# Sums over a head's 64 channels: from float32 matmuls with 64x64 blocks to two float32r passes with a 128x128 block matrix, the parts made by GpSimd

## The chip, the core and the metric

The kernel runs on one core of a Trainium2 chip. A core has a matrix engine (TensorE, PE in the profile), VectorE (DVE), ScalarE (ACT), GpSimd (POOL) and SyncE (SP, which only issues transfers here). They run side by side and wait for one another through semaphores; each takes its own instructions in a fixed order. The metric is the device time of one execution in microseconds (us), lower is better.

## The reference

Two layers of a bidirectional encoder on 256 tokens of width 2048. A layer normalises its input, multiplies it with one wide matrix, and feeds two groups of heads. Group A, sixteen heads of 64 channels, is the one that matters here (shortened):

```python
kk = heads(kf * k_k)
kk = kk * lax.rsqrt(jnp.maximum(jnp.sum(kk * kk, -1, keepdims=True), 1e-24))   # the key sum
...
for d, rev in enumerate((False, True)):
    decay = ...; a = jax.nn.sigmoid(...)
    kd = heads(kf * (1.0 + (a - 1.0) * k_a))
    y = y + wkv_scan(rh, heads(decay), kd, vh, kk, heads(a), rev)
    bonus = bonus + jnp.sum(rh * kd * rkf, -1, keepdims=True)                   # the bonus sum
yn = ...            # y normalised over the head's channels
out = yn + bonus * vh
```

Two sums run over the 64 channels of a head: one normalises the keys, one gives the bonus. Group B is a windowed attention. Both results are gated, joined, multiplied with an output matrix and added to the input.

## The kernel before

Channels lie on the 128 partitions and the 256 tokens along the columns. Two heads of 64 channels share the partitions, so group A is worked off in eight pairs, p = 0 to 7, in each of the two layers.

**The projections.** Every float32 product with the big matrices is made of three float32r matmuls (L290 to L292, tile `pm`): both operands are split into a float32r part `hi` and the rest `lo`, and hi·hi, hi·lo and lo·hi are summed. ScalarE makes the weight's `hi` (L220), VectorE its `lo` (L222). These matmuls form a long stream of steps, `S.run(n)`, three matmuls of 128x128 weights and 256 columns to a step.

**Windows and slots.** The rest of the work is cut into pieces and laid between the steps. A window holds 64 steps and is cut into 14 slots; at the head of a slot every generator that is due there runs one piece, then 4 or 5 steps follow. `scans(w)` lists the generators of window w with the slots in which they run. In the steady windows these are, for four different pairs at once:

- `scan_p`, pair w-1: prepares keys, decays and the bonus. It has two slot lists, here [6, 13] and [4, 5, 6, 7, 8, 9, 10, 11, 13]. In slot 4 it squares the keys (`sq`, tile `t`), in slot 6 the first list issues the key sum (`pk`) and the second then the decay factors PP and IP and the reciprocal, in slot 11 VectorE multiplies the bonus product (`km`, tile `lw`, two instructions), in slot 13 the first list issues the bonus sum (`pbn`) and the second `bv`, which reads it.
- `scan_i`, pair w-2 in all slots and pair w-3 in slots 0 and 1: inverts the 64x64 blocks of the delta rule (matmuls L866, L833 into `pq`, L875 into `pd`).
- `scan_b`, pair w-3 in slots 1 to 13 and pair w-4 in slots 1 to 4: the scan over the chunks (L923 to L953). In slot 12 it squares its output with sums (L964), VectorE adds the epsilon (`yv`, L965), GpSimd raises it to the power -0.5 (L966), and in slot 13 VectorE applies that (`ysq`).

The first pair of a layer has its own slots (`STAGE_P0`).

**What sets the order.** TensorE's order is that of the program, by hand. The other engines' order is made at build time by a planner: it follows the program with its own clock and gives an engine that comes free the ready instruction with the earliest place in the program. `high_priority(offset=n)` lets an instruction count as n places earlier: 95 for all of `scan_b` (`PRIO_B`), 40 for `lo`. The wrappers `PA` and `PV` (class `InTurn`) pin an instruction behind everything traced before it on its engine. The power at L966 goes to GpSimd directly, without such a pin. An engine stops at an instruction whose input isn't there, and everything behind it on that engine waits too.

**The head sums.** `head_sums` makes two matmuls, one for each head, 64 partitions into 64, with plain float32 operands and a 64x64 block of ones taken from the constant `bones`. Each shows as two matmul records in the profile (four for a head sum: 64 records of `pk` and 64 of `pbn` for 16 pairs).

**Tiles.** Tiles with one tag share its buffers in turn; a new one waits until the one before it in the buffer has been read. `ip` holds IP, `th` a pair's gate TH, both with one buffer. The results of head sums lie in PSUM, in a pool of two buffers that `scan_p` and `scan_i` share.

Of the kernel before, what the change touches and what calls it, by code (L numbers as in the profile page):

```python
# [9 lines left out]
F32 = mybir.dt.float32  # L10
F32R = mybir.dt.float32r
# [47 lines left out]


def _layout():
    names = ["ident", "ones", "bones", "cen", "gmf", "gmb"]
    off = {n: 128 * i for i, n in enumerate(names)}
    n = 128 * len(names)
    off["inv"] = n
    off["sgn"] = n + 1
    n += 2
    off["band"] = n
    n += 512
    off["lvl"] = n  # L70
    n += 64 * len(LEVELS)
    off["eye"] = n
    return off, n + 64
# [23 lines left out]
def make_consts():  # L97
    c = np.zeros((128, C_N), np.float32)
    r = np.arange(128)
    blk = (r[:, None] // 64 == r[None, :] // 64).astype(np.float32)  # L100
    put = lambda n, v: c.__setitem__((slice(None), slice(C_OFF[n], C_OFF[n] + v.shape[1])), v)
    put("ident", np.eye(128, dtype=np.float32))
    put("ones", np.ones((128, 128), np.float32))
    put("bones", blk)
    put("cen", np.eye(128, dtype=np.float32) - blk / 64.0)
    jj, tt = (r % 64)[:, None], np.arange(64)[None, :]
    put("gmf", np.concatenate([jj < tt, jj <= tt], 1).astype(np.float32))
    put("gmb", np.concatenate([jj > tt, jj >= tt], 1).astype(np.float32))
    band = np.zeros((128, 2, 256), np.float32)
    i, k = r[:, None], r[None, :]  # L110
    band[:, 0, 128:] = np.where(k <= i, 0.0, NEG)
    band[:, 1, :128] = np.where(k >= i, 0.0, NEG)
    put("band", band.reshape(128, 512))
    import jax.numpy as jnp

    inv = np.asarray(jnp.power(10000.0, -jnp.arange(32, dtype=jnp.float32) / 32))
    c[:, C_OFF["inv"]] = inv[r % 32]
    c[:, C_OFF["sgn"]] = np.where(r % 64 < 32, -1.0, 1.0)
    m = np.zeros((128, len(LEVELS), 2, 32), np.float32)
    row = r % 64  # L120
    cols = np.arange(64)
    for li, b in enumerate(LEVELS):
        lo = cols[(cols // b) % 2 == 0]
        up = cols[(cols // b) % 2 == 1]
        m[:, li, 0] = row[:, None] // b == lo[None, :] // b + 1
        m[:, li, 1] = row[:, None] // b == up[None, :] // b - 1
    put("lvl", m.reshape(128, -1))
    put("eye", (row[:, None] == cols[None, :]).astype(np.float32))
    return c
# [3 lines left out]
def hybrid_trunk_kernel(ctx, tc, xT, wi, wv, wo, par, fing, dup, iup, sink, pos, cst, out):  # L133
# [24 lines left out]
    def st(tag, shape, dt=F32, bufs=1):  # L158
        return sp.tile([128, *shape], dt, tag=tag, name=tag, bufs=bufs)
# [11 lines left out]
    PR = cp.tile([128, DEPTH, P_N], F32, name="PR")  # L171
    C = cp.tile([128, C_KEEP], F32, name="C")
    cc = lambda n, w=128: C[:, C_OFF[n] : C_OFF[n] + w]
    ident, ones, bones, cen = (cc(n) for n in ("ident", "ones", "bones", "cen"))
    gm = (cc("gmf"), cc("gmb"))

    def bigt(dt, name):
# [56 lines left out]
        def __getattr__(self, name):  # L234
            return lambda *a, **k: tc.keep_in_program_order(getattr(self.engine, name)(*a, **k))

    PA, PV = InTurn(A), InTurn(V)

    class Stream:

# [74 lines left out]
    MSK = cp.tile([128, NC, 64], F16, name="MSK")  # L315
    EYE, NEYE, EYE2 = (cp.tile([128, 64], F16, name=n) for n in ("EYE", "NEYE", "EYE2"))
    band = cp.tile([128, 512], BF16, name="band")
    FG = cp.tile([128, NKT], F32, name="FG")
    SK = cp.tile([128, DEPTH * 16], F32, name="SK")
    COS = cp.tile([128, T], F32, name="COS")  # L320
# [2 lines left out]
    def setup():  # L323
# [45 lines left out]
        V.memset(MSK, 1.0)  # L369
        V.memset(MSK[:, :, 0:1], 0.0)  # L370
        V.tensor_copy(band, cin[:, 0:512])
        V.tensor_copy(EYE, cin[:, 512 + 64 * NL : 576 + 64 * NL])
        V.tensor_scalar(NEYE, EYE, -1.0, None, op0=ALU.mult)
        V.tensor_scalar(EYE2, EYE, 2.0, None, op0=ALU.mult)
# [262 lines left out]
    def layer(l):  # L637
# [16 lines left out]
            PE.matmul(o, w[0], x[1], start=False, stop=False)  # L654
            PE.matmul(o, w[1], x[0], start=False, stop=True)

        def head_sums(o, x):
            for r in half:
                PE.matmul(o[r, 0:T], bones[r, r], x[r, 0:T], start=True, stop=True)

        def scan_p(p, t):
# [15 lines left out]
                PA.activation(TH[:, d * T : (d + 1) * T], pa[:, d * T : (d + 1) * T], AF.Tanh, scale=0.5, bias=dpm(NSH + 16, d * 8 + p))  # L679
            sq = st("t1", [T], bufs=3)  # L680
            PA.activation(sq, K, AF.Square, scale=prm(P_KK, p))
            KR = st("kkr", [T])
            PA.activation(KR, K, AF.Identity, scale=prm(P_KK, p))
            yield
# [46 lines left out]

            PV.tensor_tensor(km[:, 0:T], km[:, 0:T], km[:, T : 2 * T], op=ALU.add)
            PV.scalar_tensor_tensor(km[:, 0:T], km[:, 0:T], prm(P_RK, p), R, op0=ALU.mult, op1=ALU.mult)
            yield
            pb = wbank("pbn")
            head_sums(pb, km)
            yield
            t["bv"] = bv = st("bv", [T], bufs=3)
            PV.tensor_tensor(bv, pb[:, 0:T], VV, op=ALU.mult)
# [247 lines left out]
        def scans(w):  # L987

            gens = []
            prep = [(lag, at) for lag, at in enumerate(STAGE_P0) if lag == w] + [(1, at) for at in STAGE_P if w > 1]  # L990
            stages = [(4, scan_b, STAGE_B[1]), (3, scan_i, STAGE_I[1]), (3, scan_b, STAGE_B[0])]
            stages += [(lag, scan_p, at[0]) for lag, at in prep]
            stages += [(2, scan_i, STAGE_I[0])]
            stages += [(lag, scan_p, at[1]) for lag, at in prep]
            for lag, scan, at in stages:
                p = w - lag
                if 0 <= p < NP:
                    if (scan, p) not in chains:
                        chains[scan, p] = scan(p, L.ts[p])
                    gens.append((chains[scan, p], at))  # L1000
            return gens
# [210 lines left out]
```

## Time and profile before

| | |
|---|---|
| time, median of 3 runs | 1201.67 us (1200.83 to 1202.37) |
| the profiled execution: time, span | 1202.57 us, 1200.7 us |
| TensorE busy | 1171.1 us (98%) |
| VectorE, ScalarE, GpSimd busy | 903.2 us (75%), 766.5 us (64%), 19.2 us (2%) |
| matmuls of `pk` and `pbn` (L659) | 64 + 64 records, mean 402 ns |
| mean granted TensorE clock | 0.991 |

The span is from the first to the last instruction. The durations of matmuls overlap, since one begins while the one before it drains; the time that a matmul costs the stream is the distance between starts. "Idle before" is the time in which an engine had nothing to do ahead of an instruction, and behind the arrow stands what ended it. L235 is the line of the wrapper `InTurn`, so instructions with that line are told apart by their tiles.

### The profile page before, as it was taken

The page shows a single profiled execution, that of the slowest core. Times are in us where ns is not written, and L with a number is a line of the kernel's source. Part 1 is how long each engine was busy: PE and PEld are TensorE (multiplying, and loading weights), DVE is VectorE, ACT ScalarE, POOL GpSimd, SP SyncE. Part 2 cuts the span into 40 slices and gives each one's busy share as a digit, 9 for nine tenths or more (in the row PEclk, how much of TensorE's full clock was granted, in tenths as well). Part 3 has the DMA queues.
Part 4 walks back from the last instruction along what each step waited for, and adds up shares of the span by engine and source line. Part 5 has one row for each costly group of instructions (what it writes and reads, how often), then busy time and mean ns, then how long its engine had stood idle before and what let it go on. Part 6 is the DMA issues. An engine that isn't in the chain of part 4 may idle for free. (4 is left out here: it accounts for less than half of the span.)

```text
span 1200.7 us, 38176 instructions
## 1 busy us (share of the span) xinstructions
PE 1171.1 (98%) x16215; PEld 1088.0 (91%) x16215; DVE 903.2 (75%) x1987; ACT 766.5 (64%) x1920; POOL 19.2 (2%) x23
## 2 busy tenths in 40 slices
PE   8999999999999999999999999999999999999996
PEld 6988999999998889999999889999999988899996
DVE  6979778887877568866668878877887766786554
ACT  6756776776676557655555766776677665665553
POOL 0000000000000000000000000000000000000000
PEclk9999999999999999999999999999999999999998
DMA  7453233233323333477655343233323334345653
GB/s 270 148 169 123 97 101 127 92 112 114 108 93 118 120 114 131 143 236 235 211 187 172 124 131 113 91 114 114 111 96 105 117 120 133 113 148 184 211 186 122
DMA packets 60122, 166.71 MB, mean 139 GB/s; under 512 B 7696, under 2 KB 22704, under 8 KB 59952
## 3 DMA queue, kind: packets, MB, share of 16 engines
q1 hardware_dynamic: 59952, 164.27, 41.3%
q8 instruction: 127, 2.08, 0.7%
q14 instruction: 43, 0.35, 0.1%
HBM read 157.43 MB, written 4.19 MB: 135 GB/s over the span
## 5 line engine op out<-in xcount | busy, mean ns | idle before, releaser
L290 PE MATMUL pm<-XH,hi 128*128 128x256 f32 x1664 | 495.3, 298 | 2.4 <-ACT XH L182 2.1
L292 PE MATMUL pm<-XH,lo 128*128 128x256 f32 x1664 | 468.8, 282 | 4.8 <-DVE lo L222 4.8
L291 PE MATMUL pm<-XL,hi 128*128 128x256 f32 x1664 | 468.7, 282 | 0.3
L220 ACT ACTIVATE hi<-raw 128x512 fp32r<-128x512 f32 x560 | 327.9, 625 | 211.1 <-PE pm L291 137.5
L222 DVE TENSOR_TENSOR lo<-raw,hi 128x512 fp32r<-128x512 f32 x560 | 369.9, 687 | 100.8 <-ACT hi L220 93.9
L290 PEld LDWEIGHTS pm<-XH,hi 128*128 128x128 f32 x1664 | 314.6, 189 | 18.3 <-ACT XH L182 2.7
L292 PEld LDWEIGHTS pm<-XH,lo 128*128 128x128 f32 x1664 | 314.7, 189 | 6.5 <-DVE lo L222 6.4
L291 PEld LDWEIGHTS pm<-XL,hi 128*128 128x128 f32 x1664 | 315.1, 189 | 1.0 <-DVE XL L183 1.0
L290 PE MATMUL pm<-MH,hi 128*128 128x256 f32 x512 | 144.0, 281 | 0.0
L292 PE MATMUL pm<-MH,lo 128*128 128x256 f32 x512 | 143.8, 281 | 0.0
L291 PE MATMUL pm<-ML,hi 128*128 128x256 f32 x512 | 143.8, 281 | 0.0
L290 PEld LDWEIGHTS pm<-MH,hi 128*128 128x128 f32 x512 | 96.6, 189 | 0.8 <-issue 0.8
L292 PEld LDWEIGHTS pm<-MH,lo 128*128 128x128 f32 x512 | 96.6, 189 | 0.0
L291 PEld LDWEIGHTS pm<-ML,hi 128*128 128x128 f32 x512 | 96.6, 189 | 0.0
L869 ACT ACTIVATE QF<-pq 128x256 f16<-128x256 f32 x80 | 30.8, 385 | 25.0 <-PE pq L833 24.5
L876 DVE CAST_PREDICATED tv<-LV,pd 128x256 f16<-128x256 uint8 x80 | 34.3, 429 | 10.8 <-PE pd L875 10.0
L759 DVE TENSOR_TENSOR ge<-pg,C 128x1024 f32<-128x1024 f32 x32 | 39.1, 1221 | 3.9 <-PE pg L753 3.8
L941 ACT ACTIVATE suv<-pcc 64x128 f32<-64x128 f32 x128 | 34.2, 267 | 10.4 <-PE pcc L939 6.9
L1031 ACT ACTIVATE mv<-mv,mx 128x257 f32<-128x257 f32 x64 | 31.8, 501 | 11.5 <-DVE mx L1028 11.4
L925 ACT ACTIVATE rh<-pcc 128x128 f32<-128x128 f32 x64 | 17.5, 273 | 32.6 <-PE pcc L923 32.2
L753 PE MATMUL pg<-mv,bk 64*128 64x128 f32 x512 | 37.2, 285 | 0.0
L875 PE MATMUL pd<-QF,tt 64*64 64x32 f16 x1280 | 35.4, 186 | 0.9 <-ACT tt L837 0.8
(244 smaller groups left out, 1857.9 us busy)
## 6 DMA issues: line engine op xcount, KB each, us to landing
raw<-wi SPq DMA_DIRECT2D x208, 512.0 KB, 3.3
raw<-wo SPq DMA_DIRECT2D x64, 512.0 KB, 4.4
raw<-wv SPq DMA_DIRECT2D x8, 512.0 KB, 3.4
rrot<-u SPq DMA_DIRECT2D x80, 32.0 KB, 1.9
X<-xT SPq DMA_DIRECT2D x4, 512.0 KB, 7.1
vg<-xT SPq DMA_DIRECT2D x16, 128.0 KB, 3.6
xd<-vg SPq DMA_DIRECT2D x16, 128.0 KB, 3.5
vg<-xd SPq DMA_DIRECT2D x16, 128.0 KB, 3.3
```

Of the source, the lines that this page charges most:

```text
L220: A.activation(hi[:, q], raw[:, q], AF.Copy)
L222: V.tensor_tensor(lo[:, q], raw[:, q], hi[:, q].bitcast(F32), op=ALU.subtract)
L290: PE.matmul(pm, wh, rh[:, kk, :], start=(kk == 0), stop=False)
L291: PE.matmul(pm, wh, rl[:, kk, :], start=False, stop=False)
L292: PE.matmul(pm, wl, rh[:, kk, :], start=False, stop=(kk == 15))
L753: PE.matmul(pg[:, h, c * 128 : (c + 1) * 128], BK[half[h], d, c, 1 - h : 3 - h, :].rearrange("p s j -> p (s j)"), MV[half[h], d, c].rearra ...
L759: V.tensor_tensor(GEd(d), pg.rearrange("p h (c x) -> p h c x", c=NC), gm[d].unsqueeze(1).unsqueeze(1).to_broadcast([128, 2, NC, 128]), op= ...
L869: A.activation(t_sub(QF), flat4(pq[:, :, 0:128]), AF.Copy)
L875: PE.matmul(narrow(pd[:, d], h, c), hx(TT, d, c, h), sub(QF, h ^ d, d, c, d * b), start=True, stop=True)
L876: V.copy_predicated(t_sub(TC), t_mask, flat4(pd[:, :, 0:128]))
L941: A.activation(here(h), pc[half[h], 1], AF.Copy)
L1031: A.activation(Sc[:, h, q, 0:257], Sc[:, h, q, 0:257], AF.Exp, scale=0.125, bias=mx[:, q : q + 1], accum_out=den[:, q : q + 1])
```

## The change

The block matrix of ones leaves the constants and becomes a float32r tile `BONES` of 128x128, zero outside the two 64x64 blocks, built once by ScalarE. A head sum is now two matmuls over all 128 partitions, accumulated in the same place: the block matrix with the float32r part of the input, then with the rest. A new function `parts` makes these two on GpSimd, a copy that rounds to float32r and a subtract that reads the copy, through a new wrapper `PG` that pins them behind what was traced before on GpSimd. The parts of the squared keys are made in slot 4 in tag `ip`, those of the bonus product in slot 11 in tag `th`. In `scans`, the first slot list of `scan_p`, which holds the two head sums, moves in front of `scan_b` and the older `scan_i`.

```diff
-    names = ["ident", "ones", "bones", "cen", "gmf", "gmb"]
+    names = ["ident", "ones", "cen", "gmf", "gmb"]
...
-    PA, PV = InTurn(A), InTurn(V)
+    PA, PV, PG = InTurn(A), InTurn(V), InTurn(G)
...
+    BONES = cp.tile([128, 128], F32R, name="BONES")
...
+        A.activation(BONES, ones, AF.Copy, scale=0.0)
+        for r in half:
+            A.activation(BONES[r, r], ones[r, r], AF.Copy)
...
-        def head_sums(o, x):
-            for r in half:
-                PE.matmul(o[r, 0:T], bones[r, r], x[r, 0:T], start=True, stop=True)
+        def parts(x, tag):
+
+            hl = st(tag, [2, T], F32R)
+            PG.tensor_copy(hl[:, 0], x)
+            PG.tensor_tensor(hl[:, 1], x, hl[:, 0].bitcast(F32), op=ALU.subtract)
+            return hl
+
+        def head_sums(o, hl):
+            for i in range(2):
+                PE.matmul(o[:, 0:T], BONES, hl[:, i], start=(i == 0), stop=(i == 1))
...
             PA.activation(sq, K, AF.Square, scale=prm(P_KK, p))
+            sq = parts(sq, "ip")
...
             PV.scalar_tensor_tensor(km[:, 0:T], km[:, 0:T], prm(P_RK, p), R, op0=ALU.mult, op1=ALU.mult)
+            bonus = parts(km[:, 0:T], "th")
             yield
             pb = wbank("pbn")
-            head_sums(pb, km)
+            head_sums(pb, bonus)
...
-            stages = [(4, scan_b, STAGE_B[1]), (3, scan_i, STAGE_I[1]), (3, scan_b, STAGE_B[0])]
-            stages += [(lag, scan_p, at[0]) for lag, at in prep]
+            stages = [(lag, scan_p, at[0]) for lag, at in prep]
+            stages += [(4, scan_b, STAGE_B[1]), (3, scan_i, STAGE_I[1]), (3, scan_b, STAGE_B[0])]
             stages += [(2, scan_i, STAGE_I[0])]
             stages += [(lag, scan_p, at[1]) for lag, at in prep]
```

More of the change, by code (lines that the diff above doesn't have):

```diff
@@ L103, in make_consts @@
     put("ones", np.ones((128, 128), np.float32))
-    put("bones", blk)
     put("cen", np.eye(128, dtype=np.float32) - blk / 64.0)
@@ L173, in hybrid_trunk_kernel @@
     cc = lambda n, w=128: C[:, C_OFF[n] : C_OFF[n] + w]
-    ident, ones, bones, cen = (cc(n) for n in ("ident", "ones", "bones", "cen"))
+    ident, ones, cen = (cc(n) for n in ("ident", "ones", "cen"))
     gm = (cc("gmf"), cc("gmb"))
```

## The prediction

> **What bounds the kernel now.** I read the page's engine line first, then the time by stretches (stretch, its length, busy time and instructions of PE, PEld, DVE, ACT, POOL, granted clock, DMA share, GB/s), then what TensorE waited for.
>
> ```profile
> PE 1171.1 (98%) x16215; PEld 1088.0 (91%) x16215; DVE 903.2 (75%) x1987; ACT 766.5 (64%) x1920; POOL 19.2 (2%) x23
> ```
> ```profile
> 0.00:50.00 50.00, 45.01 (x325) 40.67 (x326) 40.50 (x102) 32.05 (x63) 1.55 (x5) 0.97 0.68 228
> 50.00:135.00 85.00, 81.18 (x1060) 74.58 (x1060) 70.18 (x139) 58.59 (x125) 0.00 (x0) 0.98 0.40 132
> 135.00:370.00 235.00, 234.32 (x4310) 214.00 (x4311) 189.38 (x388) 162.87 (x440) 6.04 (x6) 1.00 0.33 108
> ```
> ```profile
> PE pm L292 <- DVE lo L222: 4.8, 8, 1.2
> PE pq L856 <- ACT suv L794: 3.6, 2, 2.1
> ```
>
> In the windows with head sums (135 to 370 us; layer two repeats them from 725) TensorE is busy 99.7% of the time at full clock, and the largest waits of the whole span are 4.8 and 3.6 us. It takes its instructions in the program's order. So time taken off TensorE shortens the kernel one for one, and a wait put in front of one of its matmuls lengthens it one for one. VectorE (81% there) and ScalarE (69%) come second; GpSimd is nearly idle.
>
> **Part 1, the matmuls.** The cost of a head sum is read from start to start of the projection's matmuls around it, because their durations overlap. TensorE's timeline (start, duration), with the bonus sum and, at another place, the same group without it:
>
> ```profile
> 195.36 0.28 PE L292 MATMUL pm<-XH,lo 128*128 128x256 f32 x1
> 195.56 0.43 PE L659 MATMUL pbn<-lw,C 64*64 64x256 f32 x2
> ...
> 196.25 0.39 PE L290 MATMUL pm<-XH,hi 128*128 128x256 f32 x1
> ```
> ```profile
> 99.19 0.28 PE L291 MATMUL pm<-XL,hi 128*128 128x256 f32 x1
> 99.31 0.28 PE L292 MATMUL pm<-XH,lo 128*128 128x256 f32 x1
> 99.52 0.30 PE L875 MATMUL pd<-QF,tt 64*64 64x32 f16 x16
> 99.76 0.38 PE L290 MATMUL pm<-XH,hi 128*128 128x256 f32 x1
> ```
>
> 196.25 - 195.36 = 0.89 with, 99.76 - 99.31 = 0.45 without: the sum costs 0.45 us (0.455 with unrounded starts). The key sum likewise, with the same neighbours:
>
> ```profile
> 176.23 0.28 PE L292 MATMUL pm<-XH,lo 128*128 128x256 f32 x1
> ...
> 177.87 0.39 PE L290 MATMUL pm<-XH,hi 128*128 128x256 f32 x1
> ```
> ```profile
> 382.98 0.28 PE L292 MATMUL pm<-XH,lo 128*128 128x256 f32 x1
> ...
> 384.17 0.39 PE L290 MATMUL pm<-XH,hi 128*128 128x256 f32 x1
> ```
> ```profile
> 56.40 0.28 PE L292 MATMUL pm<-XH,lo 128*128 128x256 f32 x1
> 56.62 0.65 PE L659 MATMUL pk<-t,C 64*64 64x256 f32 x4
> 57.19 0.39 PE L290 MATMUL pm<-XH,hi 128*128 128x256 f32 x1
> ```
>
> 1.64 - 1.19 = 0.45 us. Standing alone (pair 0 of each layer) it costs 0.79 - 0.12 = 0.67, with the change of matmul form before and behind it. The new sum is two matmuls of the projection's form, 128x128 weights and 256 columns in float32r; those start 0.12 us apart (99.19 to 99.31; 0.117 unrounded). At the head of the slot they directly follow such matmuls, so I price the pair at 0.234 us. The gain is 0.22 us in 30 places and 0.44 in the two that stand alone: 6.6 + 0.9 = 7.5 us. It falls on the engine that sets the end.
>
> **Part 2, the order in the slot.** Only the head sums move: they are the only steps in the first slot list of `scan_p`. For the key sum (slot 6) it passes the scan's L946 and L953, starting at 176.35 rather than 177.05. The bonus sum (slot 13) already stands first on TensorE; without a change of form before it, it is due at 195.36 + 0.12 = 195.48 rather than 195.56. No DMA moves and no SyncE work. The factor IP now uses the tile that the key parts held, so on ScalarE it waits for the key sum, with the weight splits queued behind it.
>
> ```profile
> 173.43 0.52 ACT L235 ACTIVATE t<-kr,PR 128x256 f32<-128x256 f32 x1
> ```
> ```profile
> 179.16 0.63 ACT L235 ACTIVATE ip<-lw 128x512 f32<-128x512 f32 x1
> ```
>
> The key sum ends near 176.9 in the new order, over 2 us before that, so the wait costs nothing; what hides it is that IP comes late. Building BONES is three small ScalarE copies in a stretch where ScalarE is busy 32 of 50 us: nothing.
>
> **Part 3, the parts on GpSimd.** Each head sum now needs a copy and a dependent subtract of 128x256. Nothing in the trace shows GpSimd at that size. What it shows is:
>
> ```profile
> L966 POOL TENSOR_TENSOR yv<-yv,mhalf 128x4 f32<-128x4 f32 x16 | 16.3, 1017 | 815.3 <-DVE yv L965 815.3
> ...
> L1204 POOL MEMSET const-float32-1.0<- 128x1 f32 x1 | 0.1, 98 | 0.0
> ```
> ```profile
> 193.21 0.41 DVE L235 TENSOR_TENSOR lw<-lw 128x256 f32<-128x256 f32 x1
> 193.54 0.68 DVE L222 TENSOR_TENSOR lo<-raw,hi 128x512 fp32r<-128x512 f32 x1
> 194.14 0.48 DVE L235 SCALAR_TENSOR_TENSOR lw<-lw,PR,kr 128x256 f32<-128x256 f32 x1
> 194.54 0.16 DVE L965 TENSOR_SCALAR yv<-yv 128x4 f32<-128x4 f32 x1
> 195.89 0.42 DVE L235 TENSOR_TENSOR ysq<-py,yv 128x256 f32<-128x256 f32 x1 [1.19 <-POOL yv L966]
> ```
> ```profile
> 194.85 1.01 POOL L966 TENSOR_TENSOR yv<-yv,mhalf 128x4 f32<-128x4 f32 x1 [40.55 <-DVE yv L965]
> ```
>
> The bounds of one GpSimd instruction are 0.10 us (the memset) and 1.02 (the power; a power costs more per element than a copy, which is the reason to go lower). Nearest in shape is VectorE's 0.41 on the same tile. I take 0.45 for the copy and 0.60 for the subtract, which reads two tiles. Handing over costs 0.15 from VectorE to GpSimd (194.70 to 194.85) and about 0.05 back.
>
> The key parts have room: their square ends at 173.95 and the sum is due at 176.35, 2.4 us for a chain of 0.15 + 1.05 + 0.05 = 1.25. The bonus parts have not. Their input is ready at 194.62, the sum is due at 195.48: 0.86 us for 1.25. Between them stands the power of the group norm. Its input is ready 0.08 us later (194.70), it isn't pinned to the program's order, and it counts as 95 places earlier, while its place is only some 30 instructions behind the parts. A planner that hands a free engine the most urgent ready instruction gives it to GpSimd as soon as the copy ends, ahead of the subtract. The VectorE rows show it doing just this: a `lo` of higher urgency (193.54) stands between the two dependent `lw` instructions. So I expect copy, power, subtract: 194.62 + 0.15 + 0.45 + 1.02 + 0.60 + 0.05 = 196.89, and TensorE stands still 1.41 us at 195.48. All its later work of the window is queued behind that matmul. The pattern is the same in ten windows; the first and the last of them:
>
> ```profile
> 152.64 0.48 DVE L235 SCALAR_TENSOR_TENSOR lw<-lw,PR,kr 128x256 f32<-128x256 f32 x1
> 153.04 0.17 DVE L965 TENSOR_SCALAR yv<-yv 128x4 f32<-128x4 f32 x1
> ```
> ```profile
> 154.09 0.43 PE L659 MATMUL pbn<-lw,C 64*64 64x256 f32 x2
> ```
> ```profile
> 904.37 0.48 DVE L235 SCALAR_TENSOR_TENSOR lw<-lw,PR,kr 128x256 f32<-128x256 f32 x1
> 904.76 0.16 DVE L965 TENSOR_SCALAR yv<-yv 128x4 f32<-128x4 f32 x1
> ```
> ```profile
> 905.81 0.43 PE L659 MATMUL pbn<-lw,C 64*64 64x256 f32 x2
> ```
>
> In the other six no power comes near or (pair 7) it comes 0.7 us later; of these only pair 0 of layer one is short, with its input ready at 81.59 and the sum due at 81.79:
>
> ```profile
> 81.10 0.48 DVE L235 SCALAR_TENSOR_TENSOR lw<-lw,PR,kr 128x256 f32<-128x256 f32 x1
> ```
> ```profile
> 81.88 0.65 PE L659 MATMUL pbn<-lw,C 64*64 64x256 f32 x4
> ```
>
> That is 1.25 - 0.20 = 1.05 us. The power itself is 0.37 us late, with `ysq` and the splits behind it on VectorE; TensorE, which is 1.41 late, covers that.
>
> **The sum.** -7.5 + 10 x 1.41 + 1.05 = +7.7 us. The profiled execution took 1202.57 us around its span of 1200.7; that gives 1210.3, and since it lies 0.9 above the median of 1201.67, 1209.4 on the median's footing.
>
> The Trainium skill (GPSIMD Engine Reference, section on performance versus the Vector engine) gives a two-input elementwise instruction there about twice VectorE's time, 4497 against 2293 ns at 2048 columns. By it the subtract is an estimated 0.8 us rather than 0.6, each stall 0.2 longer, and the sum 1211.6; no run here shows it yet.
>
> **Rivals.**
>
> *The subtract before the power.* If the planner sees the power's input only after the copy has ended, the subtract follows at once and the matmul waits 1.25 - 0.86 = 0.39 us: -7.5 + 3.9 + 1.05 = -2.6, 1199.1 on the median's footing, not slower. It decides from a power ready over 0.45 us behind the bonus product; the rows have 0.08. For it: what orders the build is the planner's own clock, which no row shows.
>
> *No stall.* If copy and subtract take 0.33 us each or less, or the bonus product comes earlier on VectorE, only pair 0 stalls, by some 0.7: 1194.9. Against it: that is shorter than VectorE's 0.41 on this tile; for it, the memset's 0.10 and that a few changed instructions may reorder VectorE.
>
> *VectorE held off while GpSimd works.* If the two can't read at the same time, 16 x 2 x 1.05 = 34 us are taken from VectorE. In the steady windows 19% of it is free. In 50 to 135 and its copy in layer two it is busy 83% and TensorE already waits for `lo`; four parts there in each layer cost up to 8 x 1.05 = 8.4 us on top of the forecast: 1217.8. Against: at the bonus parts VectorE is idle, waiting for the power (1.19 us before `ysq`). The Trainium skill has such a rule (SBUF — State Buffer, section on the two separate sides): VectorE with two SBUF inputs and GpSimd exclude each other for a whole instruction. No run here shows it.
>
> *The passes are not cheaper.* Were the new pair as dear as the old sums, the forecast's stalls alone would make 1217; the projection's rows speak against it.
>
> **How the numbers follow.** Chances: forecast 0.48, subtract first 0.24, no stall 0.18, VectorE held off 0.08, passes dear 0.02. The forecast's own range, from the copy and subtract at 0.41 to 1.02 each, is 1207 to 1222; with the memset's 0.10 it would fall to 1200. For 8 in 10 I go from 1195 to 1218. A measurement of this kernel tells about 0.2% (2.4 us) from no change. The first rival lies on that bound, so its 0.24 is split: faster 0.12 + 0.18 = 0.30, same 0.12 + 0.03 for an edge of the forecast = 0.15, slower 0.55.
>
> **What would show it.** Right: `pbn` matmuls 0.12 us apart; TensorE waiting for GpSimd some 1.4 us at each of ten bonus sums, and GpSimd's order copy, power, subtract there; no wait at the key sums. Wrong: the power behind the subtract, GpSimd's pair well under 0.8 us, waits of TensorE for `lo` or `tv` in the steady windows, or a bonus product that VectorE finishes earlier.

## The result, and the profile after

| | before | after |
|---|---|---|
| median | 1201.25 us of 4 runs (1200.63 to 1202.37) | 1213.52 us of 4 runs (1212.81 to 1213.61) |
| the profiled execution: time, span | 1202.57 us, 1200.7 us | 1213.52 us, 1211.7 us |

The changed kernel is slower: ratio 1.010, 95% interval 1.0086 to 1.0113. The span grew by 11.0 us. (Before has one run more here than when the prediction was made.)

The engine line of the changed kernel's page, and the same three stretches of time as in the prediction, with the same columns:

```profile
PE 1166.0 (96%) x16151; PEld 1084.9 (90%) x16151; DVE 904.8 (75%) x1987; ACT 767.3 (63%) x1923; POOL 56.4 (5%) x87
```
```profile
0.00:50.00 50.00, 44.30 (x319) 40.41 (x320) 39.62 (x101) 31.99 (x64) 1.69 (x6) 0.93 0.61 216
50.00:135.00 85.00, 79.67 (x1054) 74.02 (x1053) 71.96 (x140) 58.94 (x125) 6.07 (x10) 1.00 0.42 139
135.00:370.00 235.00, 229.37 (x4152) 209.33 (x4151) 186.30 (x383) 161.35 (x436) 18.28 (x28) 1.00 0.32 105
```

TensorE has 5 us less to do and the span is 11 us longer: it stands still for 16 us more. In the third stretch, the steady windows, it was busy 234.32 of 235 us and is now busy 229.37, at the same clock of 1.00. The largest waits of the whole span (engine and matmul, what ended the wait, us in total, times, longest us):

```profile
PE pm L291 <- DVE lo L221: 6.7, 10, 1.7
PE pf L845 <- DVE tv L888: 6.5, 14, 1.6
PE pcc L958 <- ACT suv L953: 3.8, 2, 2.1
PE pbn L669 <- POOL th L234: 3.7, 13, 0.4
```

Two of the four, `pf` and `pbn`, are new in the steady windows. The bonus sum (`pbn`) waits for GpSimd, as forecast, but for 0.4 us at most, not for 1.4. And `pf`, the first matmul group of the next window, waits for VectorE's `tv`; before the change that wait stood there three times with 2.8 us in all. The timeline of one bonus sum shows how the two hang together (start, duration, engine, line, what; in brackets the idle time before it and its end):

```profile
237.37 0.48 DVE L234 SCALAR_TENSOR_TENSOR lw<-lw,PR,kr 128x256 f32<-128x256 f32 x1
237.76 0.16 DVE L977 TENSOR_SCALAR yv<-yv 128x4 f32<-128x4 f32 x1
...
238.00 0.40 POOL L234 CAST th<-lw 128x256 fp32r<-128x256 f32 x1 [19.46 <-DVE yv L977]
...
238.48 0.73 POOL L234 TENSOR_TENSOR th<-lw,th 128x256 fp32r<-128x256 f32 x1
...
238.69 0.28 PE L669 MATMUL pbn<-th,BONES 128*128 128x256 f32 x1
239.16 1.01 POOL L978 TENSOR_TENSOR yv<-yv,mhalf 128x4 f32<-128x4 f32 x1
...
239.26 0.38 PE L669 MATMUL pbn<-th,BONES 128*128 128x256 f32 x1 [0.29 <-POOL th L234]
...
240.21 0.42 DVE L234 TENSOR_TENSOR ysq<-py,yv 128x256 f32<-128x256 f32 x1 [2.29 <-POOL yv L978]
...
240.55 1.28 DVE L221 TENSOR_TENSOR lo<-raw,hi 128x512 fp32r<-128x512 f32 x2
...
241.75 0.41 DVE L888 CAST_PREDICATED tv<-LV,pd 128x256 f16<-128x256 uint8 x1
...
242.22 0.30 PE L845 MATMUL pf<-EYE,tv 64*64 64x32 f16 x16 [0.38 <-DVE tv L888]
```

The same place of the kernel before, one row for each that was moved:

```profile
236.01 0.16 DVE L965 TENSOR_SCALAR yv<-yv 128x4 f32<-128x4 f32 x1
237.36 0.42 DVE L235 TENSOR_TENSOR ysq<-py,yv 128x256 f32<-128x256 f32 x1 [1.18 <-POOL yv L966]
237.70 1.28 DVE L222 TENSOR_TENSOR lo<-raw,hi 128x512 fp32r<-128x512 f32 x2
238.90 0.42 DVE L876 CAST_PREDICATED tv<-LV,pd 128x256 f16<-128x256 uint8 x1
```
```profile
237.06 0.43 PE L659 MATMUL pbn<-lw,C 64*64 64x256 f32 x2
...
239.70 0.30 PE L833 MATMUL pf<-EYE,tv 64*64 64x32 f16 x16
```

On GpSimd the order is copy, subtract, power. The first pass of the bonus sum starts on time, because the copy is ready; the second waits for the subtract. The power comes last, 1.10 us later than before: from `yv` to `ysq` it is 240.21 - 237.76 = 2.45 us, and was 237.36 - 236.01 = 1.35. Behind `ysq` on VectorE stand two `lo` and then `tv`. In the kernel before, `tv` ended 0.38 us ahead of `pf` (238.90 + 0.42 to 239.70); now `pf` waits for it. So one slow engine delays TensorE twice in a window, once through the subtract and once through the power.

The durations on GpSimd (group; behind the bar busy us and mean ns of one, then the idle time before):

```profile
L978 POOL TENSOR_TENSOR yv<-yv,mhalf 128x4 f32<-128x4 f32 x16 | 16.4, 1025 | 156.8 <-DVE yv L977 156.7
L234 POOL TENSOR_TENSOR th<-lw,th 128x256 fp32r<-128x256 f32 x16 | 12.1, 754 | 1.3
L234 POOL CAST th<-lw 128x256 fp32r<-128x256 f32 x16 | 6.8, 422 | 323.5 <-DVE yv L977 194.7 <-DVE lw L234 110.1 <-PE pq L845 18.8
```

The key sum of a steady window costs what was forecast, 178.70 - 177.28 = 1.42 us for its group against 1.64, and it waits for nobody:

```profile
177.28 0.28 PE L291 MATMUL pm<-XH,lo 128*128 128x256 f32 x1
177.39 0.40 PE L669 MATMUL pk<-ip,BONES 128*128 128x256 f32 x2
...
178.70 0.38 PE L289 MATMUL pm<-XH,hi 128*128 128x256 f32 x1
```

**Where the 11 us are.** The table gives, for a group of TensorE's work, the time from the start of the last projection matmul ahead of it to the start of the first one behind it, as the median over the windows (12 for the key sum, 14 for the others); the labels are those of the experiments below.

| us per window | key sum (slot 6) | `pq` in slot 10 | `py` in slot 12 | bonus sum (slot 13) | `pf`, next window |
|---|---|---|---|---|---|
| before | 1.64 | 0.95 | 1.16 | 0.90 | 1.94 |
| after | 1.42 | 0.95 | 1.32 | 1.23 | 2.39 |
| e1_key_only | 1.42 | 0.95 | 1.33 | 0.90 | 1.94 |
| e2_bonus_only | 1.76 | 0.95 | 0.95 | 1.22 | 2.39 |
| e3_parts_unread | 1.76 | 0.95 | 0.95 | 0.90 | 2.71 |
| e4_power_first | 1.42 | 0.95 | 1.31 | 2.67 | 2.24 |
| e5_parts_act_dve | 1.42 | 1.30 | 0.96 | 1.87 | 1.94 |
| e7_move_only | 1.76 | 0.95 | 0.95 | 0.90 | 1.93 |
| e9_key_one_pass | 1.30 | 1.20 | 0.95 | 0.90 | 1.94 |
| e10_one_pass | 1.30 | 1.04 | 0.95 | 0.56 | 1.94 |
| e11_no_power | 1.42 | 0.99 | 1.33 | 1.22 | 1.94 |
| e12_vector_relief | 1.42 | 0.95 | 0.95 | 0.90 | 1.93 |

From before to after a window gains 0.22 at the key sum and loses 0.15 in slot 12, 0.33 at the bonus sum and 0.45 at `pf`: 0.7 us, and 7.4 us over the ten steady windows of both layers (measured from start to start of the projection's steps 226 and 546 of each layer: +3.71 and +3.68). The other 3.6 us lie at the starts and ends of the layers. The same division for every run, as the growth of the profiled span over that of before (steps are counted over all projection matmuls with the layer's input, `pm` and `pva`; each row rests on one traced execution):

| us | ten steady windows | starts and ends | span |
|---|---|---|---|
| after | +7.4 | +3.6 | +11.0 |
| e1_key_only | -0.9 | +2.8 | +1.9 |
| e2_bonus_only | +6.6 | +3.2 | +9.7 |
| e3_parts_unread | +6.6 | -1.2 | +5.4 |
| e4_power_first | +28.9 | +8.0 | +36.9 |
| e5_parts_act_dve | +8.5 | +7.2 | +15.7 |
| e6_later_sum | +18.0 | +18.6 | +36.6 |
| e7_move_only | -1.2 | -3.1 | -4.3 |
| e8_bonus_later | +18.3 | +10.7 | +29.0 |
| e9_key_one_pass | -3.0 | -0.2 | -3.2 |
| e10_one_pass | -8.3 | +9.5 | +1.2 |
| e11_no_power | +2.9 | +6.3 | +9.2 |
| e12_vector_relief | -5.0 | -0.9 | -5.9 |

TensorE's granted clock has a part in these columns. In every trace it falls to 0.50 for spells of 3.4 or 6.8 us, and a spell costs at most half its length. Outside the steady windows, up to the last projection matmul, the spells come to 5.1 us of full clock in before (they start at 8.8, 87.3 and 408.1 us), 3.4 in after, 8.5 in e6, e10 and e11, and 1.7 in e3 and e12. Inside the steady windows only e4 has any. So differences of 2 or 3 us in the middle column can be the clock of one execution, and not the kernel: e10's ten executions have spans from 1195.8 us at a mean clock of 0.994 to 1202.3 at 0.988, and the traced one took 1201.9.

### The profile page after: what moved, and what is told of

The parts are those of the page before. It is cut to its first block, busy times and chain, and to the rows that moved or that the text cites. A ratio compares the mean times of both kernels' runs of the same rounds, so it can differ in the third digit from the quotient of the medians.

```text
span 1211.7 us, 38148 instructions
## 1 busy us (share of the span) xinstructions
PE 1166.0 (96%) x16151; PEld 1084.9 (90%) x16151; DVE 904.8 (75%) x1987; ACT 767.3 (63%) x1923; POOL 56.4 (5%) x87
## 5 line engine op out<-in xcount | busy, mean ns | idle before, releaser
L765 PEld LDWEIGHTS pg<-mv,bk 64*128 64x128 f32 x512 | 31.1, 187 | 2.0
```

Source lines behind the costliest of these rows:

```text
L765: PE.matmul(pg[:, h, c * 128 : (c + 1) * 128], BK[half[h], d, c, 1 - h : 3 - h, :].rearrange("p s j -> p (s j)"), MV[half[h], d, c].rearra ...
```

## The experiments

Unless it says otherwise, the diff is against the changed kernel. Where a sum goes back to the old form, it uses a function that makes two float32 matmuls with 64x64 blocks, as before, read from BONES:

```diff
+        def head_sums32(o, x):
+            ones32 = BONES.bitcast(F32)
+            for r in half:
+                PE.matmul(o[r, 0:T], ones32[r, r], x[r, 0:T], start=True, stop=True)
```

### One sum at a time

**e1_key_only:** the key sum in the new form, the bonus sum in the old one, without parts.

```diff
-            bonus = parts(km[:, 0:T], "th")
             yield
             pb = wbank("pbn")
-            head_sums(pb, bonus)
+            head_sums32(pb, km)
```

> The key sum in two float32r passes with GpSimd parts and at the head of its slot, the bonus sum as before (float32, 64x64 blocks). Theory: the whole loss comes from the bonus parts on GpSimd (TensorE waits for the subtract, and the power behind the parts holds VectorE), so without them the key sums' gain stays: 12 x 0.22 + 2 x 0.22 + 2 x 0.44 = 4.0 us under the kernel before, about 1197.3, and no wait of TensorE for a GpSimd result or, at the head of a window, for tv. Rival: GpSimd's parts slow VectorE wherever they stand, or the 0.16 us that the changed kernel loses in slot 12 is the key sum's gain given back to a late ScalarE: then 1199 to 1201, with the 0.16 in slot 12 of every window.

Measured: 1204.44 us (median of 10), ratio 1.0023 (1.0013 to 1.0033). In the steady windows the key sum gains its 0.22 us and neither the bonus sum nor `pf` waits, but 0.17 of it is lost again in slot 12. The rest of the loss, +3.75 us, lies at the end of layer two, where this execution had a spell of half clock from 981.9 to 985.3 us (up to 1.7 us). So the cheaper key sum alone doesn't make the kernel faster; what happens in slot 12 is taken up under e12.

**e2_bonus_only:** the reverse, the key sum old and without parts, the bonus sum new.

```diff
-            sq = parts(sq, "ip")
...
-            head_sums(pk, sq)
+            head_sums32(pk, sq)
```

> The bonus sum in two float32r passes with GpSimd parts, the key sum as before (float32, 64x64 blocks), at the head of its slot. Theory: all waits of the changed kernel stay and only the key sums' gain is lost: 1213.5 + 4.0 = 1217.5, with 0.45 us at the second pass of the bonus sum and 0.45 us at the head of the next window. Rival (the loss is spread over both sums): 1207 to 1210.

Measured: 1210.1 us (median of 4), ratio 1.0074 (1.0054 to 1.0093). The bonus sum and `pf` lose 0.32 and 0.45 us, the same as in the full change: the loss comes with the bonus parts. Two more things show that were not expected. A float32 key sum at the head of its slot costs 0.12 us more (1.76 against 1.64). There it stands between a projection matmul and the scan's float32 ones; in the kernel before it stood behind these, and its records alternate with those of `pq`. Which of the two makes the 0.12 us no run separates. In exchange slot 12 gets 0.21 us shorter.

### Which of GpSimd's two delays costs what

**e3_parts_unread:** both sums old, GpSimd still makes the bonus parts and nobody reads them. Only the power's delay is left.

```diff
-            sq = parts(sq, "ip")
...
-            bonus = parts(km[:, 0:T], "th")
+            parts(km[:, 0:T], "th")
...
-            head_sums(pb, bonus)
+            head_sums32(pb, km)
```

> Both head sums as before; GpSimd makes the bonus parts, but no one reads them. Theory: TensorE then has nothing to wait for at the bonus sum, but the power still starts 1.2 us late behind the parts, VectorE stands at the normalisation, and tv comes late: 0.45 us at the head of the next window and some 0.15 in slot 12, ten to twelve times: 1207 to 1209. Rival: the matmul's wait for the subtract is the only cause, and the late tv follows from that wait: 1201 to 1202.

Measured: 1208.05 us (median of 5), ratio 1.0054 (1.0035 to 1.0072). The bonus sum is back at 0.90 us and waits for nothing. The wait of TensorE that grew:

```profile
PE pf L849 <- DVE tv L892: 10.4, 14, 1.3
```

Each window loses 0.77 us at `pf` (1.94 to 2.71). The late power costs this by itself, more than in the full change, where TensorE reaches `pf` 0.33 us later anyway and so waits 0.33 us less.

**e11_no_power:** the other way round: the parts are read, and the power is left out. In its place VectorE multiplies the same 128x4 tile, so the group norm is scaled by another number.

```diff
-            G.tensor_tensor(yv, yv, mhalf, op=ALU.pow)
+            V.tensor_tensor(yv, yv, mhalf, op=ALU.mult)
```

> As the changed kernel, but the power on GpSimd is left out and a multiplication of the same 128x4 on VectorE stands in its place (the group norm is scaled by another number). Theory: with nothing of VectorE's behind the parts on GpSimd, the normalisation is over 2 us earlier and the wait for tv at the head of the next window goes: -0.45 x 12 = 5.4 us, perhaps the 0.16 in slot 12 too; the wait at the bonus sum stays: 1205 to 1208. Rival (the parts hold VectorE itself, or tv is late because the bonus sum is): the wait for tv stays, 1211 to 1214.

Measured: 1210.44 us (median of 4), ratio 1.0071 (1.0046 to 1.0095). TensorE's waits, both lines of it:

```profile
PE pf L845 <- DVE tv L888: 4.8, 4, 1.9
...
PE pbn L669 <- POOL th L234: 3.6, 13, 0.4
```

The bonus sum's wait stays as it was (3.7 in the changed kernel, 3.6 here). `pf` no longer waits in the steady windows, 4 times in all instead of 14, and its group is back at 1.94: -0.45 us a window, as the theory has it. The total fell by less than expected, because the ends and starts of the layers lost 2.7 us more; this trace's spells of half clock there are worth up to 5.1 us more than after's, which would cover it. With e3, the two delays are told apart: the subtract costs the bonus sum 0.55 us (0.33 net of the 0.22 that its matmuls gain), the power costs `pf` 0.45.

**e4_power_first:** the power ahead of the subtract. Traced one slot later, both parts fall behind the power on GpSimd. (The prediction had the copy first, then the power and the subtract; no run built that order, though the expectation below takes this one for it.)

```diff
-            bonus = parts(km[:, 0:T], "th")
             yield
+            bonus = parts(km[:, 0:T], "th")
             pb = wbank("pbn")
```

> As the changed kernel, but the bonus parts are traced in slot 13, so on GpSimd they stand behind the power: power, copy, subtract. This is the order that the forecast expected. Theory: the power and VectorE are on time, the wait for tv at the head of the next window goes (-0.45 to -0.6 x 12), but the bonus sum waits for power 1.02 + copy 0.42 + subtract 0.75: about 1.6 us after it is due, 1.0 more than in the changed kernel, ten times: 1216 to 1219. Rival (the wait for tv doesn't come from the power): it stays and the time is 1222 to 1225.

Measured: 1239.47 us (median of 4), ratio 1.0314 (1.0293 to 1.0335). Here the order is power, copy, subtract. One bonus sum, by GpSimd, VectorE and TensorE:

```profile
242.04 1.01 POOL L978 TENSOR_TENSOR yv<-yv,mhalf 128x4 f32<-128x4 f32 x1 [19.47 <-DVE yv L977]
243.00 0.40 POOL L234 CAST th<-lw 128x256 fp32r<-128x256 f32 x1
243.48 1.21 POOL L234 TENSOR_TENSOR th<-lw,th 128x256 fp32r<-128x256 f32 x1
```
```profile
243.08 0.42 DVE L234 TENSOR_TENSOR ysq<-py,yv 128x256 f32<-128x256 f32 x1 [1.12 <-POOL yv L978]
243.42 1.81 DVE L221 TENSOR_TENSOR lo<-raw,hi 128x512 fp32r<-128x512 f32 x2
```
```profile
243.45 0.39 PE L669 MATMUL pbn<-th,BONES 128*128 128x256 f32 x1 [0.56 <-POOL th L234]
...
244.74 0.38 PE L669 MATMUL pbn<-th,BONES 128*128 128x256 f32 x1 [0.90 <-POOL th L234]
```

The group of the bonus sum takes 2.67 us: 1.77 more than before, so its waits are 1.77 + 0.22 = 1.99 us. Most of what it has over the forecast's 1.41 has a visible cause. The subtract now falls on VectorE's two `lo`, and both get longer: the subtract 1.21 us instead of 0.73, the pair of `lo` 1.81 instead of 1.28. `tv` is done in time all the same, and in the steady windows `pf` waits for nothing: with the power on time the wait for `tv` is gone, as in e11. The order that the changed kernel really has is thus much cheaper than this one.

What looks like a loss at `pf` (2.24 in the table) is the clock. In eight of the ten steady windows it falls to half for 3.4 us right behind the bonus sum, here from 246.1 us, and the projection's matmuls then start 0.21 us apart instead of 0.12:

```profile
245.42 0.42 DVE L888 CAST_PREDICATED tv<-LV,pd 128x256 f16<-128x256 uint8 x1 [0.18 <-PE pd L887]
```
```profile
245.64 0.28 PE L291 MATMUL pm<-XH,lo 128*128 128x256 f32 x1
245.76 0.28 PE L289 MATMUL pm<-XH,hi 128*128 128x256 f32 x1
...
246.56 0.41 PE L291 MATMUL pm<-XH,lo 128*128 128x256 f32 x1
246.78 0.41 PE L289 MATMUL pm<-XH,hi 128*128 128x256 f32 x1
...
248.19 0.40 PE L845 MATMUL pf<-EYE,tv 64*64 64x32 f16 x16
```

The two windows without such a spell grew by 1.74 us each and have `pf` at 1.94, the eight with one by some 3.2: about 11 of the 28.9 us of the steady windows are the clock. No other run has a spell there, and each begins within 1 us of the end of the bonus sum with its two waits. So the long waits seem to bring it on; no run tests that.

### Other ways to make the parts

**e5_parts_act_dve:** the copy on ScalarE, the subtract on VectorE; GpSimd has only its power.

```diff
-            PG.tensor_copy(hl[:, 0], x)
-            PG.tensor_tensor(hl[:, 1], x, hl[:, 0].bitcast(F32), op=ALU.subtract)
+            PA.activation(hl[:, 0], x, AF.Copy)
+            PV.tensor_tensor(hl[:, 1], x, hl[:, 0].bitcast(F32), op=ALU.subtract)
```

> As the changed kernel, but the parts are made by ScalarE (copy) and VectorE (subtract) instead of GpSimd. Theory: the power is on time, so the wait for tv at the head of the next window goes (-0.45 x 12), but VectorE's full queue between slots 4 and 12 gets 0.42 us longer (slot 12 waits 0.4 more), and the bonus sum still waits about 0.4 for the two steps: 1208 to 1213, no better than GpSimd's. Rival (GpSimd itself, by its slowness and its hold on VectorE, is the cause): 1195 to 1200.

Measured: 1216.67 us (median of 4), ratio 1.0121 (1.0102 to 1.014), worse than with GpSimd. Its waits:

```profile
PE pbn L669 <- DVE th L234: 9.3, 10, 1.0
...
PE pq L878 <- DVE tv L888: 4.1, 12, 0.8
```

`pf` is well again (1.94), so GpSimd's power is indeed what had delayed it. But the bonus sum waits longer, now for parts that ScalarE and VectorE make in turn among their other work, and VectorE's extra work shows as a wait for `tv` in slot 10.

**e6_later_sum** and **e8_bonus_later** give the parts time: they are made behind the power, the bonus sum follows in slot 2 of the next window and its reader in slot 3. e6 keeps the new key sum, e8 has the old one in its old place. The common part of the diff:

```diff
-STAGE_P = (([6, 13], [4, 5, 6, 7, 8, 9, 10, 11, 13]),)
-STAGE_P0 = (([], [12, 13]), ([3], [3, 5, 6, 8, 10]), ([2], [0, 3]))
+STAGE_P = (([6], [4, 5, 6, 7, 8, 9, 10, 11, 13]), ([2], [3]))
+STAGE_P0 = (([], [12, 13]), ([3], [3, 5, 6, 8, 10]), ([3], [0, 1, 4]))
...
+            yield
             bonus = parts(km[:, 0:T], "th")
             yield
             pb = wbank("pbn")
```

> As the changed kernel, but the bonus parts are made behind the power (slot 13) and the bonus sum moves to slot 2 of the next window, its reader bv to slot 3. Theory: no wait for the subtract and no late power: a steady window gains 0.22 at the bonus sum and 0.06 net at the key sum, about 3 us over the kernel; what the key-only kernel lost at the ends of the layers (some 3.5 us) may remain: 1198 to 1203. Rival (the bonus parts hold VectorE wherever they stand): the parts now run beside the weight splits, and slower splits or tv make TensorE wait again: 1206 to 1212.

> The bonus sum alone in the new form, its parts behind the power and the sum in slot 2 of the next window; the key sum in float32 and at its old place in slot 6. Theory: the bonus sum's gain stays, 14 x 0.22 = 3 us, and GpSimd no longer slows VectorE's full stretch at the key parts: 1197 to 1200, below the kernel before. Rival as in the run with both sums: 1204 to 1210.

Measured: 1238.24 us (median of 4), ratio 1.0294 (1.0271 to 1.0317), and 1231.62 us (median of 4), ratio 1.0253 (1.0229 to 1.0277). The two lines of e6 that say why:

```profile
PE pq L869 <- ACT suv L807: 24.7, 16, 2.9
PE pf L846 <- DVE tv L889: 11.6, 14, 2.1
```

The bonus sum has no wait any more, but two new ones stand in its place. It now holds one of the two PSUM buffers that `scan_p` and `scan_i` share, just when `pq` of slot 3 needs one, and each window loses 1.46 us there (both kernels). And the parts now run beside VectorE's `lo`, as in e4, so `tv` is late and `pf` loses 0.6 us. So in this layout the time that the parts were given was taken from `pq`, through the buffer.

### What the cheaper matmuls are worth

**e7_move_only:** the kernel before, with nothing but the first slot list of `scan_p` moved to the head of the slot. The diff is against the kernel before.

```diff
-            stages = [(4, scan_b, STAGE_B[1]), (3, scan_i, STAGE_I[1]), (3, scan_b, STAGE_B[0])]
-            stages += [(lag, scan_p, at[0]) for lag, at in prep]
+            stages = [(lag, scan_p, at[0]) for lag, at in prep]
+            stages += [(4, scan_b, STAGE_B[1]), (3, scan_i, STAGE_I[1]), (3, scan_b, STAGE_B[0])]
```

> The kernel before with the head sums at the head of their slot and nothing else. Theory: the key sum then stands between a projection matmul and the scan's float32 matmuls and costs 0.12 us more in slot 6 (a change of form more), and slot 12, where TensorE waits some 0.2 us for ScalarE's suv, takes that back: within 1.5 us of the kernel before. Rival (the move is what disturbs the ends of the layers, where the key-only kernel lost some 3 us): 1203 to 1206.

Measured: 1198.88 us (median of 10), ratio 0.998 (0.9969 to 0.9991): faster than both kernels, if only by 0.2%. Part 2 of the change is no loss. The form change costs 0.12 us at the key sum, slot 12 gives 0.21 back, and 3 of the 4 us come from the layers' starts and ends.

**e9_key_one_pass:** e1 with the second pass of the key sum left out; the rests of the squared keys are still made and not added.

```diff
-            for i in range(2):
-                PE.matmul(o[:, 0:T], BONES, hl[:, i], start=(i == 0), stop=(i == 1))
+            PE.matmul(o[:, 0:T], BONES, hl[:, 0], start=True, stop=True)
```

> As the kernel with the key sum alone in the new form, but the key sum's second pass is left out on TensorE (the rest of the squared keys isn't added; GpSimd still makes it). That takes 0.12 us more off TensorE in slot 6 of 16 pairs. Theory: between slot 4 and slot 12 VectorE's queue sets the pace, so what TensorE saves there comes back as a longer wait for ScalarE's suv in slot 12: no gain in the steady windows, the time within 0.6 us of 1204.4, and the group with the second half of the scan in slot 12 grows from 1.33 to about 1.45 us. Rival: TensorE sets the pace there and the loss of the key-only kernel is all at the ends of the layers: 16 x 0.12 = 1.9 us less, 1202.5.

Measured: 1201.74 us (median of 10), ratio 1.0003 (0.999 to 1.0017). One pass is worth 0.12 us, as the distance of the projection's matmuls says. The wait in slot 12 is gone and one of 0.25 us has come in slot 10, for VectorE's `tv`. At first this looked like evidence against VectorE as what holds up slot 12. The rows of ScalarE say otherwise: here its `tt` stands ahead of its `bk`, in e1 behind it, so `suv` comes about 0.4 us (the length of `tt`) earlier for a reason of its own, and the lag shows two slots sooner instead.

**e10_one_pass:** both sums as one float32r pass over an input that ScalarE or VectorE rounds as it writes it. No parts on GpSimd; the rests are not added.

```diff
-            for i in range(2):
-                PE.matmul(o[:, 0:T], BONES, hl[:, i], start=(i == 0), stop=(i == 1))
+            PE.matmul(o[:, 0:T], BONES, hl, start=True, stop=True)
...
-            sq = st("t1", [T], bufs=3)
+            sq = st("t1", [T], F32R, bufs=3)
...
-            sq = parts(sq, "ip")
...
-            PV.scalar_tensor_tensor(km[:, 0:T], km[:, 0:T], prm(P_RK, p), R, op0=ALU.mult, op1=ALU.mult)
-            bonus = parts(km[:, 0:T], "th")
+            bonus = st("th", [T], F32R)
+            PV.scalar_tensor_tensor(bonus, km[:, 0:T], prm(P_RK, p), R, op0=ALU.mult, op1=ALU.mult)
```

> As the changed kernel, but each head sum is one float32r pass over an input that ScalarE or VectorE rounds to float32r as it writes it; the rest of the input isn't added and GpSimd makes no parts. TensorE saves 0.45 - 0.12 = 0.34 us in 30 places and 0.55 in two: 11 us. Theory: the bonus sum's half (14 x 0.34 = 4.7) reaches the end, since nothing of it waits for GpSimd; of the key sum's 4 us most comes back as a longer wait in slot 12; the ends of the layers may cost up to 3: 1193 to 1198, below both kernels. Rival (saved TensorE time is given back everywhere, because VectorE's queue sets the pace of the whole window): 1199 to 1203.

Measured: 1201.33 us (median of 10), ratio 0.9994 (0.9978 to 1.0011). With no parts to wait for, both sums give 0.34 us each (0.455 - 0.117), slot 12 gives 0.2 more, and the ten steady windows together 8.3 us. In the traced execution the starts and ends of the layers take 9.5 us back, of which the spells of half clock cover up to 3.4 (one of 6.8 us begins at 675.5); the rest is not explained. So the forecast's price for a pass holds, and even a change that wins everywhere in the steady windows can be lost at the layers' ends.

**e12_vector_relief:** is it VectorE's pace that gives the key sum's gain back in slot 12? In e1, VectorE works without a gap from `tv` in slot 4 to `u` in slot 11, 15.3 us. This kernel is e1 with two of VectorE's subtracts in that stretch (the rests of the low-rank weights) replaced by ScalarE copies times zero; these rests are left out of the result.

```diff
-                    PV.tensor_tensor(lo, raw[0:rows], hi.bitcast(F32), op=ALU.subtract)
+                    PA.activation(lo, raw[0:rows], AF.Copy, scale=0.0)
```

> The key sum alone in the new form (1204.4 us), and two of VectorE's instructions of each window (the rests of the low-rank weights, `iu` and `du`, 0.41 us each in the rows, 0.33 from start to start) replaced by ScalarE copies times zero in a stretch where ScalarE stands idle for 2.1 us; the rests are left out of the result. Theory 'VectorE paces slots 5 to 12': in the kernel with the key sum alone VectorE works without a gap for 15.3 us, from its `tv` in slot 4 to the `u` of slot 11, and TensorE's scan waits in slot 12 for `suv`, which ScalarE makes behind the `bk` that it gets from VectorE. With VectorE 0.67 us shorter, `suv` comes 0.67 us earlier and the wait goes: the group in slot 12 falls from 1.33 to 0.95 us, the key sum keeps its 0.22, the whole stretch of slots 6 to 12 falls from 4.91 to about 4.53, and the steady windows gain some 0.4 us each, -2.3 us per layer's steady part against -0.4 before. Rival 'ScalarE's own order sets suv' (or GpSimd's reading holds TensorE's partner up): slot 12 stays at 1.3 and the steady part at -0.4 per layer. Starts and ends of the layers may move by some us either way under both, so the steady part decides, not the total.

Measured: 1196.07 us (median of 5), ratio 0.9962 (0.9948 to 0.9976). Slot 12 in e1, by ScalarE and TensorE, and then in e12:

```profile
230.20 0.63 ACT L234 ACTIVATE bk<-bk 64x512 f32<-64x512 f32 x1 [0.81 <-DVE bk L234]
...
232.91 0.55 ACT L957 ACTIVATE suv<-pcc 64x128 f32<-64x128 f32 x2
```
```profile
233.22 0.74 PE L969 MATMUL py<-suv,ge 128*64 128x64 f32 x8
```
```profile
231.33 0.55 ACT L957 ACTIVATE suv<-pcc 64x128 f32<-64x128 f32 x2
```
```profile
232.37 0.45 PE L969 MATMUL py<-suv,ge 128*64 128x64 f32 x8
```

In e1 ScalarE waits for VectorE's `bk`, `suv` starts 0.31 us ahead of `py` and is not ready when its second half is needed, so `py` stretches to 0.74 us. In e12 `suv` starts 1.04 us ahead and `py` takes 0.45. The group falls from 1.33 to 0.95 us, all other groups stay, and the steady windows gain 2.50 us a layer (2.3 were expected, 0.44 with e1). Two things changed at once: counted from the start of the group in slot 12, ScalarE's `bk`, which waits for VectorE, begins 0.41 us earlier than in e1, and ScalarE's `tt` went ahead of it, as in e9, which brings `suv` another 0.41 us. For slot 12 the second alone is enough, as e9 shows, where the group takes 0.95 us too; but e9, whose key sum is 0.12 us shorter still, then waits 0.25 us in slot 10, and e12 doesn't. That is probably what VectorE's relief adds; no run has it alone. GpSimd's key parts are not what fills VectorE there: in e7, without them, the stretch from `tv` to `u` takes 15.27 us.

## Why the prediction was right or wrong

**The time.** 1209.4 us was forecast, 1213.5 measured, inside the range and on the forecast side. The way there was partly another one.

**Part 1, right in size, wrong in what becomes of it.** A sum gains 0.22 us, one that stands alone 0.44 (0.79 to 0.35), and a pass costs 0.12 us. What failed is the sentence that the gain "falls on the engine that sets the end". At the key sums TensorE reaches slot 12 earlier, waits there for `suv`, and loses 0.15 to 0.17 of the 0.22 us; in e12 it keeps them, with less work on VectorE and another order on ScalarE. TensorE's share of 99.7% hid that in slots 6 to 12 VectorE and ScalarE were only just in time. Of the 7.5 us that the prediction counted, the steady key sums kept about 0.7 (ten times 0.07).

**Part 2, right.** The key sums wait for nobody, IP's later start and BONES cost nothing that can be seen, and e7 shows that the order in the slot is no loss.

**Part 3, the durations nearly right, the order wrong.** The copy took 0.40 us (0.45 taken), the subtract 0.73 undisturbed (0.60 taken), the handing over 0.15 as read. The estimate from the Trainium skill (GPSIMD Engine Reference, section on performance versus the Vector engine) was 0.8 for the subtract; 0.73 lies nearer to it than to the 0.60 that was taken.

The step that failed is "so I expect copy, power, subtract". GpSimd did copy, subtract, power, the order of the first rival. The argument from VectorE's `lo` between two dependent `lw` did not carry over to GpSimd; why the build put the subtract first was not found. The stall at the bonus sum is 0.55 us, not 1.41.

The second step that failed is "the power itself is 0.37 us late; TensorE, which is 1.41 late, covers that". With the real order the power is 1.10 us late and TensorE only 0.55, and the difference reaches TensorE through `ysq`, `lo` and `tv` at `pf`: 0.45 us a window, shown by e3 and e11. The first rival had the order right and lacked this term; with the measured 0.55 and 0.45 in it, it would have come to -7.5 + 10 x 1.00 + 1.05 = +3.6 us. The remaining difference to +11 is the key sums' gain that slot 12 took back (1.5) and the layers' starts and ends: +3.6 us, where the sum had -2.1 (gains of 12 sums, 3.1, less the 1.05 of pair 0).

So it was luck that the forecast came near: a stall of 1.41 us at one place stood for 0.55 + 0.45 + 0.15 at three, and 5.7 us more at the starts and ends of the layers, which the sum didn't have, made up the difference. Its own order was not built. In the nearest, e4, where the copy too stands behind the power, TensorE waits 1.99 us at the bonus sum; the span grows by 37 us, of which the spells of half clock in the steady windows are about 11. That the subtract and `lo` slow each other down, and that long waits may lower the clock, the sum had at nothing.

**The other rivals.** "No stall" fell: the pair takes 1.16 us on GpSimd (238.00 to the start of the power at 239.16). "VectorE held off" is no cause of the loss at the bonus parts, as the prediction argued: VectorE stands idle there for 2.29 us. At the key parts it is not held up to speak of (15.30 us from `tv` to `u` with them in e1, 15.27 without in e7). It does act where the two meet, in e4 and e6. "The passes are not cheaper" fell with the key sum's row.

**What stays open.** The starts and ends of the layers moved by -3.1 to +18.6 us between kernels. Part of that is the clock, up to 3.4 us either way against before; the planner makes its orders anew for every change, and how much comes of that was not measured. In e6 and e8 they share the cause of the steady windows; in after, e1 and e10 no single one was found.

## What to carry to other kernels

Before work goes to an engine that is nearly idle, list what urgent work it already has and who waits behind that: here 1.1 us more on GpSimd cost TensorE once through its own result and once through the power queued behind it. Cheaper work on the busiest engine is worth only what the next wait leaves of it, so look how close to late each of its inputs already is, window by window, and not only at its busy share. Where a build lays out the orders, judge a change by the part of the kernel that repeats, measure the ends separately, and look at the granted clock before a loss is put down to a wait.

## What the runs showed of the hardware that was not expected

VectorE and GpSimd slow each other down, but only in some pairings. Beside GpSimd's subtract, the 128x512 split `lo` (both inputs in SBUF) took 1.81 us for two instead of 1.28, and the subtract 1.21 us instead of 0.73 (e4). `ysq`, which reads one input from PSUM, ran beside GpSimd's copy in e4 and took its usual 0.42 us. The Trainium skill (SBUF — State Buffer, section on the two separate sides) has VectorE with two SBUF inputs and a GpSimd instruction that reads SBUF exclude each other; these rows agree, with a loss of 0.5 us on each side, and `ysq` with its one SBUF input went free. One SBUF input alone doesn't decide it, though: VectorE's `lw` (TENSOR_SCALAR, 128x512, one input) took 0.57 us (median) with the key parts in the changed kernel, and 0.42 in e7, which has no parts.

The cost of a matmul sum depends on its neighbours: the same float32 key sum takes 0.12 us more at the head of its slot, between a projection matmul and the scan's float32 ones, than behind these, where it alternates with `pq` (1.76 against 1.64 us, e7 against before).

A wait of TensorE may cost more than its length. In e4, with about 2 us of waits at the bonus sum, the granted clock fell to 0.50 for 3.4 us behind it in eight of ten steady windows, some 1.4 us each; with 0.55 us of waits there, in the changed kernel, it never did. That the one brings on the other is argued from this coincidence alone.
